# A first stage rewritten around one pass per tile: scaling, squares and h without GpSimd arithmetic

## The chip, the cores and the metric

The kernel runs on one core of one Trainium2 chip. The metric is the device time of one execution in microseconds (us), lower is better; it is given as the median of several runs. Engines are named as in the profile: PE (TensorE matmul) and PEld (its weight load), DVE (VectorE), ACT (ScalarE), POOL (GpSimd), SP (SyncE, which here only issues transfers).

## The reference: what is computed

One layer of a hybrid decoder for a prompt of 1024 tokens and 8 samples of 8 tokens (1088 tokens in all), width 1024, all in fp32. Cut to what the change touches:

```
mod = silu(c) @ w_mod + b_mod
shift, scale, gate = split(mod, 3)
h = rmsnorm(x, norm_g) * (1 + scale) + shift
proj = h @ w_in                      # columns mg, u, va, za, q, k, v, o, z, gates, p, zc
...                                  # three token mixers, gated and merged
x = x + gate * (merged @ w_out);  y = rmsnorm(x, final_norm_g)
```

The prompt has one c, so one shift and scale a channel; each sample has its own, so there are nine columns of them (`[:, 0]` for the prompt, `[:, 1:9]` for the samples).

## The kernel before, in words

Activations lie transposed: channels on the 128 partitions (8 tiles, index k), the T = 1088 tokens along the free dimension, the 1024 prompt tokens first (`TP`), then the 64 of the samples (`smp`). Every fp32 product is made of three products of fp32r parts: a number is split into a high part (a cast, on ACT) and a low part (the number minus its high part, on DVE), and high x high, high x low and low x high are summed. `split` is this pair of operations. A panel is 256 columns of a weight matrix; `Stream` brings its four pieces (128x512) by SP and splits them (`step`: `whi` on ACT, L132, `wlo` on DVE, L101).

The first stage (`start`) works before shift and scale are known. It writes q = ((x * am) @ w) * r + shift @ w, where am is norm_g * (1 + scale) and r the reciprocal root mean square of a token. So panels q0 and q1 are multiplied with x * am, without r and shift; these are put in afterwards. Meanwhile r is computed, and h = x * am * r + shift is built, for panels q2, q3 and all that follow.

The order of all this is written by hand: `PLAN_0` and `PLAN_1` are strings whose letters name operations, and each engine carries out its instructions in the order in which the letters issue them. The letters: `1` load of a panel of w_mod (1 MB in slots of 128x1024), `2` load of an x tile (544 KB), `3` load of a weight piece, `w` a few dummy matmuls, `S` split of half a w_mod panel (`ssh`, `ssl`), `M` its product with the silu(c) columns `scs` (16 matmuls, L548), `C` copy out of PSUM (L554), `T` turn into am or sm (shift) columns (L564, L569, L571), `Q` square of an x tile (L577, L580) and its addition to `acc` (POOL, L581), `A`/`V` scaling of x by am in place (samples L586, prompt on ACT L588 or DVE L590), `H`/`L` high and low part of the scaled x (L595, L601), `W` split of a weight piece, `P`/`R` high and low passes of one x tile against q0 or q1 (12 and 6 matmuls, L614), `e` sum of squares over channels (matmuls L625) and r (`rs`; its power runs on POOL, L217, the refinement on DVE), `f` r spread over partitions (`rb`, L641, L644), `v`/`g` x * rb on DVE or POOL (L648), `m` high and low part of h with the shift added on the way (L653 to L660; the upper halves of the first four tiles are also stored to `b12d`), `z`/`s`/`t` the product shift @ w for q0 and q1 (L668 to L690), `r` the raw sums out of PSUM into rows (L698, L700).

The pool of SBUF slots has 34 buffers of 128x1088; x tiles, splits, h and rows all live there. PSUM has 8 banks in this stage.

After the plan come panels q2 (`b_panel`, six sums of 24 matmuls, L270) and q3. In q3 (`kouter=True`) the loop over k is the outer one: six sums fill six banks and are copied out together at the end (`evac_rows`, L859). Beside the two panels run generators, one step at a time (`tick`): `finish_rows` multiplies the rows of q0 and q1 by rb on POOL (L705), adds the shift term and stores them; `gen_factors` prepares right-hand factors for the panels after them. Those (`seven_panels`, matmuls L362) are computed with seven half-size products for eight; their factors t1 to t4 are sums and differences of quarters of h, which `gen_factors` first puts together again as hh + hl (`fac`, L765). `put_t4` overwrites the upper half of h's first four tiles with the fourth of them. Later, `gen_gate` multiplies silu(c) (`self.scs`, kept since the start) with the last third of w_mod.

Of the kernel before, what the change touches and what calls it, by code (L numbers as in the profile page):

```python
# [16 lines left out]
TP = 1024  # L17
# [141 lines left out]
class Builder:  # L159
# [98 lines left out]
    def b_panel(self, panel, acts, evac, nk=KT, kouter=False, hook=None):  # L258
# [3 lines left out]
        units = [(f, g) for f in range(2) for g in range(3)]  # L262
# [22 lines left out]
        for u, (f, g) in enumerate(units):  # L285
            p = self.ps()
            for k in range(nk):
                mms(p, f, g, k)
                if k == nk // 2 - 1:
                    self.tick(self.pace / 2)  # L290
            evac(f, g, p[:, : GROUPS[g][1]])
            self.prep_some(panel, u, len(units))
            self.tick(self.pace / 2)
        self.st.used(panel)
# [171 lines left out]
    def start(self):  # L466
# [10 lines left out]
        raws, wsp, pmod, xs, xsp = {}, {}, {}, {}, {}  # L477
# [41 lines left out]
        A.copy(self.scs[:, :, 0:9], sc)  # L519
        V.tensor_tensor(out=self.scs[:, :, 32:41], in0=sc, in1=self.scs[:, :, 0:9].bitcast(F32), op=ALU.subtract)  # L520
# [9 lines left out]
        def mod_split():  # L530
            n, j = divmod(nxt("ms"), 2)
            raw = raws[n][j]
            hi = self.slot([128, 4, 256], F32R, name="ssh")
            lo = self.slot([128, 4, 256], F32R, name="ssl")
            m = 4 if n else 2
            for q in range(0, 4, m):
                self.split(*(x[:, q : q + m] for x in (raw, hi, lo)))
# [4 lines left out]
        def mod_mul():  # L542
            n = nxt("mm")
            p = pmod[n] = self.ps()
            w = wsp.pop(n)
            for kk in range(KT):
                for j in range(2):
                    PE.matmul(p[:64, :256], self.scs[:, kk, :], w[kk // 4][j][:, kk % 4, :],  # L548
                              start=(kk == 0 and j == 0), stop=(kk == KT - 1 and j == 1))
# [7 lines left out]
        def mod_turn():  # L557
# [3 lines left out]
            if n == 0:  # L561
                V.tensor_scalar(bmod[:, 1, :], bmod[:, 1, :], 1.0, None, ALU.add)
            for j in range(2):
                PE.matmul(p[:, j * 16 : j * 16 + 9], t[:, j * 128 : j * 128 + 128], sel, start=True, stop=True)  # L564
# [8 lines left out]
        def square():  # L573
# [4 lines left out]
            else:  # L578
                sq = self.slot([128, T], name="sq")
                A.activation(sq, xs[k], AF.Square)  # L580
                G.tensor_tensor(out=acc[0], in0=acc[0], in1=sq, op=ALU.add)  # L581

        def x_scale(on_act):
            k = nxt("xa")
            x = xs[k]
            V.tensor_tensor(out=bview(x[:, smp]), in0=bview(x[:, smp]), in1=bcol(am[:, k, 1:9]), op=ALU.mult)  # L586
            if on_act:
                A.activation(x[:, :TP], x[:, :TP], AF.Copy, scale=am[:, k, 0:1])  # L588
            else:
                V.tensor_scalar(x[:, :TP], x[:, :TP], am[:, k, 0:1], None, ALU.mult)  # L590

        def x_high():
            k = nxt("xh")
            hi = self.slot([128, T], F32R, name="xhi")
            A.copy(hi, xs[k])  # L595
            xsp[k] = [hi, None]

        def x_low():
            k = nxt("xlo")
            lo = self.slot([128, T], F32R, name="xlo")  # L600
            V.tensor_tensor(out=lo, in0=xs[k], in1=xsp[k][0].bitcast(F32), op=ALU.subtract)  # L601
            xsp[k][1] = lo

        def mms(part):
# [13 lines left out]
            if n == KT - 1 and part == "low":  # L618
                self.st.units -= 4

        def rms_sum():
            p = self.ps()
            for t in range(9):
                m = 128 if t < 8 else 64
                PE.matmul(p[:m, t : t + 1], acc[0][:, t * 128 : t * 128 + m], ones, start=True, stop=True)  # L625
            ms = self.const([128, 9], "ms")
# [5 lines left out]
            acc.clear()  # L632

        def rms_rows():
            rb.append(self.slot([128, T], name="rb"))
            for b in range(3):
                p = self.ps()
                n = 0
                for t in range(4 * b, min(9, 4 * b + 4)):
                    m = 128 if t < 8 else 64  # L640
                    PE.matmul(p[:, n : n + m], rs[:m, t : t + 1].to_broadcast([m, 128]), self.ident[:m, :m],  # L641
                              start=True, stop=True)
                    n += m
                A.copy(rb[0][:, b * 512 : b * 512 + n], p[:, :n])  # L644

        def h_scale(eng):
            x = xs[nxt("hs")]
            eng.tensor_tensor(out=x, in0=x, in1=rb[0], op=ALU.mult)  # L648

        def h_make():  # L650
            k = nxt("hm")
            x = xs.pop(k)
            V.tensor_tensor(out=bview(x[:, smp]), in0=bview(x[:, smp]), in1=bcol(sm[:, k, 1:9]), op=ALU.add)  # L653
            hh = self.slot([128, T], F32R, name="hhi")
            hl = self.slot([128, T], F32R, name="hlo")
            A.activation(hh[:, :TP], x[:, :TP], AF.Identity, bias=sm[:, k, 0:1])
            A.copy(hh[:, smp], x[:, smp])
            V.scalar_tensor_tensor(out=hl[:, :TP], in0=x[:, :TP], scalar=sm[:, k, 0:1], in1=hh[:, :TP].bitcast(F32),
                                   op0=ALU.add, op1=ALU.subtract)
            V.tensor_tensor(out=hl[:, smp], in0=x[:, smp], in1=hh[:, smp].bitcast(F32), op=ALU.subtract)  # L660
# [11 lines left out]
        def shift_mm():  # L672
# [20 lines left out]
        def raw_rows():  # L693
            r = [self.slot([128, T], name="row") for _ in range(2)]
            for u in range(6):
                f, (g0, n) = u // 3, GROUPS[u % 3]
                if u % 2:
                    V.tensor_copy(r[f][:, g0 : g0 + n], sums[-1][u][:, :n])  # L698
                else:
                    A.copy(r[f][:, g0 : g0 + n], sums[-1][u][:, :n])  # L700
            rows.append(r)

        def finish_rows(n):
            for f in range(2):
                G.tensor_tensor(out=rows[n][f], in0=rows[n][f], in1=rb[0], op=ALU.mult)  # L705
# [8 lines left out]
            if n:  # L714
# [3 lines left out]
        def late_const():  # L718
            self.ident = self.cload("ident")

        ops = {
            "1": mod_load, "2": x_load, "3": self.st.load, "4": late_const,
            "w": keep_warm, "S": mod_split, "M": mod_mul, "C": mod_copy, "T": mod_turn,
            "Q": square, "A": lambda: x_scale(True), "V": lambda: x_scale(False), "H": x_high, "L": x_low,
            "W": self.st.step, "P": lambda: mms("high"), "R": lambda: mms("low"),
            "e": rms_sum, "f": rms_rows, "v": lambda: h_scale(V), "g": lambda: h_scale(G), "m": h_make,
            "z": shift_split, "s": shift_mm, "t": shift_turn, "r": raw_rows,
        }
        self.st.ahead = 1
# [11 lines left out]
        self.drain()  # L741

        def hook(k):
            for j in range(2):
                if k == j + 1:
                    self.put_t4(j)
            if k in (1, 3):
                self.side = [self.gen_factors(2 + k // 2)]
            self.tick(2)
            if k in (5, 6):  # L750
                self.put_t4(k - 3)

        self.b_panel(self.pan["q", 3], self.h, self.evac_rows(3, self.qd), kouter=True, hook=hook)
        self.drain()
        self.pace = 1

    def gen_factors(self, j):
# [3 lines left out]
        ab = []  # L761
        for k in (j, j + 4):
            hh, hl = self.h[k]
            t = self.slot([128, T], name="fac")
            V.tensor_tensor(out=t, in0=hh.bitcast(F32), in1=hl.bitcast(F32), op=ALU.add)  # L765
            ab.append(t)
            yield
        a, b = ab
        a0, a1, b0, b1 = a[:, :W], a[:, W:], b[:, :W], b[:, W:]
        V.tensor_tensor(out=a0, in0=a1, in1=a0, op=ALU.subtract)  # L770
        V.tensor_tensor(out=a1, in0=b1, in1=a1, op=ALU.subtract)
        V.tensor_tensor(out=b1, in0=b1, in1=a0, op=ALU.subtract)
# [3 lines left out]
        self.split(a, *t13)  # L776
        if j % 2 == 0:
# [72 lines left out]
    def evac_rows(self, n, dst, scale=None):  # L850
# [3 lines left out]
        def evac(f, g, ps):  # L854
            g0, w = GROUPS[g]
            if g == 0:
                st[f] = self.slot([128, T], name="row")
            if scale is None:
                self.A.copy(st[f][:, g0 : g0 + w], ps)  # L859
            else:  # L860
                self.A.mul(st[f][:, g0 : g0 + w], ps, scale)
            if g == 2:
# [1102 lines left out]
```

## Time and profile before

| | us |
|---|---|
| median of 3 runs (lowest, highest) | 1856.58 (1855.35, 1859.59) |
| the profiled execution | 1857.86 |
| its span, first to last instruction | 1856.1 |
| busy in the span: PE, DVE, ACT, POOL | 1796.1, 1071.9, 586.0, 262.3 |
| mean granted clock of PE | 0.985 of full speed |
| panel q2 begins; the seven-product panels begin | 119.3; 176.9 |

In the rows that follow, a group row reads: line, engine, operation, output <- inputs, shapes, count, then busy us and mean ns of one, then the idle time of the engine just before these instructions and what ended it. A row of the time line or of the chain begins with the start in us and the duration. A row of stretches gives for each engine the busy time and in brackets the number of instructions, then the granted PE clock, the share of DMA engines busy and GB/s.

### The profile page before, as it was taken

What the parts mean: (1) busy time and instruction counts of PE and PEld (TensorE: products, weight loads), DVE (VectorE), ACT (ScalarE), POOL (GpSimd) and SP (SyncE); (2) the same over time, 40 slices, a digit from 0 to 9 for tenths busy, and PEclk for the clock granted to TensorE, in tenths of its full rate; (3) what the DMA queues carried; (4) which work ended last, traced back from release to release, by engine and by line L of the source; (5) the groups of instructions that cost most, each with busy time, mean ns of one, the idle gap of its engine ahead of it and who ended that gap; (6) DMA issues with size and microseconds to landing.
All of it is one profiled execution on the core that took longest, in us unless ns stands there. A gap on an engine that the chain in (4) does not pass through costs nothing.

```text
span 1856.1 us, 32242 instructions
## 1 busy us (share of the span) xinstructions
PE 1796.1 (97%) x13017; PEld 1777.4 (96%) x13017; DVE 1071.9 (58%) x2003; ACT 586.0 (32%) x1141; POOL 262.3 (14%) x427
## 2 busy tenths in 40 slices
PE   7888999999999999999999999999999999999998
PEld 7888999999999998999999899999999999999998
DVE  7777556665666542434527955664655766564444
ACT  5443333333333332222223125332333231131224
POOL 3440000000000001110011212321101101200023
PEclk8988999999999999999999999999999999999999
DMA  6332323332222334333335754776457577694422
GB/s 252 108 128 74 106 94 94 104 122 80 71 70 76 130 106 150 121 123 101 94 116 189 217 180 125 240 237 201 143 175 231 179 228 208 184 317 142 151 62 97
DMA packets 142152, 270.42 MB, mean 146 GB/s; under 512 B 19377, under 2 KB 66161, under 8 KB 142003
## 3 DMA queue, kind: packets, MB, share of 16 engines
q1 hardware_dynamic: 118786, 184.20, 31.4%
q0 software_dynamic: 23072, 83.91, 13.3%
q8 instruction: 102, 1.67, 0.4%
q14 instruction: 48, 0.39, 0.1%
q10 hardware_dynamic: 144, 0.26, 0.0%
HBM read 179.96 MB, written 88.35 MB: 145 GB/s over the span
## 4 chain that ended last, share of the span: by engine, by line
PE 86%; DVE 8%; issue 2%; DMA 2%; ACT 1%; POOL 1%; SPq 0%; POOLq 0%; DVEq 0%; ACTq 0%
PE ps L270 30%; PE ps L308 15%; PE p L362 8%; PE y L362 8%; PE z L362 8%; PE x L362 4%; PE ps L614 2%; PE ps L316 1%; PE ps L1466 1%; PE ps L1264 1%; PE ps L1485 1%; PE ps L1682 1%; PE ps L1439 1%; PE ps L1468 1%; DMA ss<-in_w_mod_dram 1%
## 5 line engine op out<-in xcount | busy, mean ns | idle before, releaser
L101 DVE TENSOR_TENSOR wlo<-raw,whi 128x512 fp32r<-128x512 f32 (+1 forms) x272 | 189.7, 698 | 115.6 <-ACT whi L132 115.6
L308 PE MATMUL ps<-whi,hhi 128*128 128x256 f32 (+1 forms) x768 | 218.5, 284 | 0.0
L308 PE MATMUL ps<-wlo,hhi 128*128 128x256 f32 (+1 forms) x768 | 216.0, 281 | 0.0
L308 PE MATMUL ps<-whi,hlo 128*128 128x256 f32 (+1 forms) x768 | 215.1, 280 | 0.0
L270 PE MATMUL ps<-hhi,whi 128*128 128x362 f32 (+1 forms) x624 | 208.2, 334 | 5.5 <-DVE C L1494 3.4
L270 PE MATMUL ps<-hlo,whi 128*128 128x362 f32 (+1 forms) x624 | 207.0, 332 | 1.9 <-DMA hlo<-b12d 1.7
L270 PE MATMUL ps<-hhi,wlo 128*128 128x362 f32 (+1 forms) x624 | 206.6, 331 | 0.0
L270 PE MATMUL ps<-yhi,whi 128*128 128x362 f32 (+1 forms) x576 | 190.1, 330 | 3.0 <-DVE mgr L1742 1.6
L270 PE MATMUL ps<-yhi,wlo 128*128 128x362 f32 (+1 forms) x576 | 188.7, 328 | 0.0
L270 PE MATMUL ps<-ylo,whi 128*128 128x362 f32 (+1 forms) x576 | 188.5, 327 | 0.0
L132 ACT CAST whi<-raw 128x512 fp32r<-128x512 f32 (+1 forms) x272 | 162.3, 617 | 44.9 <-DVE raw L123 36.3
L308 PEld LDWEIGHTS ps<-whi,hhi 128*128 128x128 f32 x768 | 144.6, 188 | 0.8 <-issue 0.4
L308 PEld LDWEIGHTS ps<-wlo,hhi 128*128 128x128 f32 x768 | 144.7, 188 | 0.0
L308 PEld LDWEIGHTS ps<-whi,hlo 128*128 128x128 f32 x768 | 144.4, 188 | 0.0
L270 PEld LDWEIGHTS ps<-hhi,whi 128*128 128x128 f32 x624 | 119.2, 191 | 6.7 <-DVE C L1494 3.6
L362 PE MATMUL p<-hhi,whi 128*128 128x272 f32 x400 | 116.1, 290 | 7.3 <-ACT row L859 7.3
L270 PEld LDWEIGHTS ps<-hlo,whi 128*128 128x128 f32 x624 | 119.5, 191 | 2.6 <-DMA hlo<-b12d 2.6
L270 PEld LDWEIGHTS ps<-hhi,wlo 128*128 128x128 f32 x624 | 119.4, 191 | 0.0
L362 PE MATMUL p<-hlo,whi 128*128 128x272 f32 x400 | 116.5, 291 | 0.0
L362 PE MATMUL p<-hhi,wlo 128*128 128x272 f32 x400 | 116.3, 291 | 0.0
L132 ACT CAST whi<-sum 128x512 fp32r<-128x512 f32 x75 | 46.6, 621 | 219.7 <-DVE sum L119 144.0
L270 PEld LDWEIGHTS ps<-yhi,whi 128*128 128x128 f32 x576 | 108.2, 188 | 3.7 <-DVE mgr L1742 1.8
(434 smaller groups left out, 4489.6 us busy)
## 6 DMA issues: line engine op xcount, KB each, us to landing
raw<-in_w_in_dram SPq DMA_DIRECT2D x204, 256.0 KB
mgr<-mgd SPq DMA_DIRECT2D x24, 544.0 KB
raw<-in_w_br_dram SPq DMA_DIRECT2D x48, 256.0 KB
out_dram<-C POOLq DMA_DIRECT2D x36, 256.0 KB, 4.5
ylo<-yd SPq DMA_DIRECT2D x16, 544.0 KB
merd<-mgr POOLq DMA_DIRECT2D x16, 544.0 KB, 6.1
C<-in_state_C_dram SPq DMA_DIRECT2D x32, 256.0 KB
mgd<-mg POOLq DMA_DIRECT2D x14, 544.0 KB, 4.6
```

Of the source, the lines that this page charges most:

```text
L101: self.kb.V.tensor_tensor(out=lo, in0=src, in1=hi.bitcast(F32), op=ALU.subtract)
L132: kb.A.copy(hi, src)
L270: self.PE.matmul(ps[:, :n], part(panel, w, k, fs), a[:, g0 : g0 + n], start=(k == 0 and j == 0), stop=(k == nk - 1 and j == 2))
L308: self.PE.matmul(p[:, :cols], a[:, ts], part(panel, w, k, cs), start=(k == 0 and j == 0), stop=(k == KT - 1 and j == 2))
L316: self.PE.matmul(p[:, :cols], stack[:, k, :], part(panel, j, k, cs), start=(k == 0 and j == 0), stop=(k == KT - 1 and j == 1))
L362: PE.matmul(bank[n][:, g, :HT], w[:, ks], b[:, gs], start=(n in (1, 5, 6, 7) and j == 0 and m == 0), stop=(j == 3 and m == 2), skip_group_ ...
L614: PE.matmul(sums[-1][u][:, :m], self.st.part(w, 1 - ww, k, fs), a[:, g0 : g0 + m], start=(k == 0 and part == "high" and j == 0), stop=(k = ...
L1264: self.PE.matmul(p[:, :n], wsl[:, ww, k, fs], a[:, g0 : g0 + n], start=(k == 0 and j == 0), stop=(k == 1 and j == 2))
L1439: PE.matmul(x["ps"][:, h * 128 : h * 128 + 128], k[:, 2 * h + d, :], q[:, 2 * h + d, :], start=(d == 0), stop=(d == 1))
L1466: PE.matmul(p[:, :258], x["qw"][:, 2 * h + d, :], C[x["hp"]][:, h, d, :], start=(d == 0), stop=False)
L1468: PE.matmul(p[:, :258], x["P"][:, a, h, :], x["vs"][:, b, h, :], start=(x["c"] == 0 and j == 0), stop=(j == 2))
L1485: PE.matmul(p[:, :258], x["ks"][:, a, h, d * 128 : d * 128 + 128], x["vs"][:, b, h, :], start=(j == 0), stop=(j == 2))
```

## The change

- x is no longer scaled in place for the prompt: `H` scales while it casts (ACT), `L` forms x * am - high in one scalar-tensor-tensor (DVE). The samples' 64 columns are scaled in place inside `H`. Letters `A` and `V` go.
- The squares are added on DVE, and each h scale is on DVE as x * am * rb in one operation; `m` adds the shift into x in fp32 (ACT) and then splits it. x stays alive as fp32 h, and `gen_factors` takes it from there, without hh + hl.
- `e` also makes the place for rb; `f` comes in two parts. The row sums of q1 are multiplied by rb while they leave PSUM (DVE), those of q0 on DVE in `finish_rows`; the turn of the shift product moves there too.
- q3 runs in the order of `b_panel` with the sums in the order 2, 1, 0, 5, 4, 3, each copied out when it is done; `put_t4` follows in a hook after each sum.
- The plan is another: loads, splits and products of a group stand together; the first w_mod panel comes in two loads, the small loads ahead of it. `gen_gate` builds its own `scs`.

```diff
         def mod_load():
-            m = 4 if n else 2
-            for j in range(0, KT, m):
-                S.dma_start(raws[n][j // 4][:, j % 4 : j % 4 + m], i["w_mod"][panels[n]][:, j : j + m, :])
+            for j in range(2):
+                S.dma_start(raws[n][j], i["w_mod"][panels[n]][:, 4 * j : 4 * j + 4, :])
...
-        cT = self.slot([128, KT, 9], name="cT")
+        cT = self.const([128, KT, 9], "cT")
         S.dma_start(cT, i["cT"])
-        mod_load()
-        sel = self.cload("sel")
         bmod = self.cload("bmodT")
         ng = self.cload("norm_gT")
...
                 A.activation(sq, xs[k], AF.Square)
-                G.tensor_tensor(out=acc[0], in0=acc[0], in1=sq, op=ALU.add)
-        def x_scale(on_act):
-            ...
+                V.tensor_tensor(out=acc[0], in0=acc[0], in1=sq, op=ALU.add)
         def x_high():
-            A.copy(hi, xs[k])
+            A.activation(hi[:, :TP], x[:, :TP], AF.Copy, scale=am[:, k, 0:1])
+            V.tensor_tensor(out=bview(x[:, smp]), in0=bview(x[:, smp]), in1=bcol(am[:, k, 1:9]), op=ALU.mult)
+            A.copy(hi[:, smp], x[:, smp])
         def x_low():
-            V.tensor_tensor(out=lo, in0=xs[k], in1=xsp[k][0].bitcast(F32), op=ALU.subtract)
+            V.scalar_tensor_tensor(out=lo[:, :TP], in0=x[:, :TP], scalar=am[:, k, 0:1], in1=hi[:, :TP].bitcast(F32),
+                                   op0=ALU.mult, op1=ALU.subtract)
+            V.tensor_tensor(out=lo[:, smp], in0=x[:, smp], in1=hi[:, smp].bitcast(F32), op=ALU.subtract)
...
-        def h_scale(eng):
-            eng.tensor_tensor(out=x, in0=x, in1=rb[0], op=ALU.mult)
+        def h_scale():
+            V.scalar_tensor_tensor(out=x[:, :TP], in0=x[:, :TP], scalar=am[:, k, 0:1], in1=rb[0][:, :TP], op0=ALU.mult,
+                                   op1=ALU.mult)
+            V.tensor_tensor(out=x[:, smp], in0=x[:, smp], in1=rb[0][:, smp], op=ALU.mult)
+            V.tensor_tensor(out=bview(x[:, smp]), in0=bview(x[:, smp]), in1=bcol(sm[:, k, 1:9]), op=ALU.add)
         def h_make():
-            x = xs.pop(k)
-            V.tensor_tensor(out=bview(x[:, smp]), in0=bview(x[:, smp]), in1=bcol(sm[:, k, 1:9]), op=ALU.add)
-            A.activation(hh[:, :TP], x[:, :TP], AF.Identity, bias=sm[:, k, 0:1])
-            A.copy(hh[:, smp], x[:, smp])
-            V.scalar_tensor_tensor(out=hl[:, :TP], in0=x[:, :TP], scalar=sm[:, k, 0:1], in1=hh[:, :TP].bitcast(F32),
-                                   op0=ALU.add, op1=ALU.subtract)
-            V.tensor_tensor(out=hl[:, smp], in0=x[:, smp], in1=hh[:, smp].bitcast(F32), op=ALU.subtract)
+            x = xs[k]
+            A.activation(x[:, :TP], x[:, :TP], AF.Identity, bias=sm[:, k, 0:1])
+            self.split(x, hh, hl)
...
         def raw_rows():
-                if u % 2:
-                    V.tensor_copy(r[f][:, g0 : g0 + n], sums[-1][u][:, :n])
+                if rows:
+                    V.tensor_tensor(out=d, in0=sums[-1][u][:, :n], in1=rb[0][:, g0 : g0 + n], op=ALU.mult)
+                elif u % 2:
+                    V.tensor_copy(d, sums[-1][u][:, :n])
...
         def finish_rows(n):
-            for f in range(2):
-                G.tensor_tensor(out=rows[n][f], in0=rows[n][f], in1=rb[0], op=ALU.mult)
+            shift_turn()
             yield
             for f in range(2):
+                if n == 0:
+                    V.tensor_tensor(out=r, in0=r, in1=rb[0], op=ALU.mult)
...
-        self.side = [finish_rows(0), finish_rows(1), self.gen_factors(0), self.gen_factors(1)]
+        self.side = [finish_rows(0), finish_rows(1)] + [self.gen_factors(j) for j in range(4)]
...
-        self.b_panel(self.pan["q", 3], self.h, self.evac_rows(3, self.qd), kouter=True, hook=hook)
+        self.b_panel(self.pan["q", 3], self.h, self.evac_rows(3, self.qd), hook=hook, order=(2, 1, 0, 5, 4, 3))
...
     def gen_factors(self, j):
-        for k in (j, j + 4):
-            hh, hl = self.h[k]
-            t = self.slot([128, T], name="fac")
-            V.tensor_tensor(out=t, in0=hh.bitcast(F32), in1=hl.bitcast(F32), op=ALU.add)
-            ...
+        a, b = self.xs.pop(j), self.xs.pop(j + 4)
...
 Builder.PLAN_0 = (
-    "wSS3w21M2W2CT1QVwSH4SL2wPQMV2Q1CWTHR21VSPHLSPMQ3Q2RVHLRLCTPVWSRHL23SPWQQMC3RVTHAHLLwPRQV3H"
-    "LPSSRPR1WS3"
+    "1223w 1223wQQSSwMCTHHWLLw SSMC1223QQTPHHWPLLRR SSMC1223QQTPHHWPLLRR SSMC13QQTPHHWPLLRR 13WPPRRe"
 )
 Builder.PLAN_1 = (
-    "rW13SeSM1CPP3MS3PCfRTSgMCgPWSvRgTMgCRTvRTPzmWRmsmgPmPWmWgPRRmtms3R3WmW3tr"
+    "r3WPR 1SSMCPRffTvm 1SSMCPRWvmPRT SSMC3vmPRWvmPRT SSMC3vmPRvmPRTzs 3vm3vmsWWWWr"
 )
```

More of the change, by code (lines that the diff above doesn't have):

```diff
@@ L255, in prep_some, with b_panel @@
                 self.st.step()
-    def b_panel(self, panel, acts, evac, nk=KT, kouter=False, hook=None):
+    def b_panel(self, panel, acts, evac, nk=KT, kouter=False, hook=None, order=(0, 1, 2, 3, 4, 5)):
         self.st.need(panel)
         part = self.st.part
-        units = [(f, g) for f in range(2) for g in range(3)]
+        units = [divmod(u, 3) for u in order]
         def mms(ps, f, g, k):
@@ L293, in b_panel @@
             self.tick(self.pace / 2)
+            if hook is not None:
+                hook(u)
         self.st.used(panel)
@@ L531, in mod_split @@
             n, j = divmod(nxt("ms"), 2)
-            raw = raws[n][j]
             hi = self.slot([128, 4, 256], F32R, name="ssh")
             lo = self.slot([128, 4, 256], F32R, name="ssl")
-            m = 4 if n else 2
-            for q in range(0, 4, m):
-                self.split(*(x[:, q : q + m] for x in (raw, hi, lo)))
+            self.split(raws[n][j], hi, lo)
             wsp.setdefault(n, []).append((hi, lo))
@@ L547, in mod_mul @@
                 for j in range(2):
-                    PE.matmul(p[:64, :256], self.scs[:, kk, :], w[kk // 4][j][:, kk % 4, :],
-                              start=(kk == 0 and j == 0), stop=(kk == KT - 1 and j == 1))
+                    PE.matmul(p[:64, :256], scs[:, kk, :], w[kk // 4][j][:, kk % 4, :], start=(kk == 0 and j == 0),
+                              stop=(kk == KT - 1 and j == 1))
         def mod_copy():
@@ L617, in mms, with rms @@
                 xsp[k] = None
-            if n == KT - 1 and part == "low":
-                self.st.units -= 4
-        def rms_sum():
+        def rms():
             p = self.ps()
@@ L631, in rms_sum @@
             self.rsqrt(rs, ms, rt)
-            acc.clear()
+            rb.append(self.slot([128, T], name="rb"))
         def rms_rows():
[L635 to L644, printed above, removed]
@@ L646, in h_scale @@
-        def h_scale(eng):
-            x = xs[nxt("hs")]
-            eng.tensor_tensor(out=x, in0=x, in1=rb[0], op=ALU.mult)
+            b = nxt("rr")
+            t0, t1 = ((0, 4), (4, 9))[b]
+            ps = [self.ps() for _ in range(-(-(t1 - t0) // 4))]
+            for t in range(t0, t1):
+                m = 128 if t < 8 else 64
+                o = (t - t0) % 4 * 128
+                PE.matmul(ps[(t - t0) // 4][:, o : o + m], rs[:m, t : t + 1].to_broadcast([m, 128]), self.ident[:m, :m],
+                          start=True, stop=True)
@@ L776, in gen_factors @@
         self.split(a, *t13)
+        yield
         if j % 2 == 0:
@@ L855, in evac @@
             g0, w = GROUPS[g]
[L856 to L862, printed above, removed]
-                self.G.dma_start(dst[2 * n + f], st.pop(f))
+            if f not in st:
+                st[f] = [self.slot([128, T], name="row"), 0]
+            self.A.copy(st[f][0][:, g0 : g0 + w], ps)
+            st[f][1] += 1
+            if st[f][1] == 3:
+                self.G.dma_start(dst[2 * n + f], st.pop(f)[0])
         return evac
@@ L882, in load @@
             return w
+        scs = self.slot([128, KT, 64], F32R, name="scs")
+        V.tensor_copy(scs, self.zero.unsqueeze(1).to_broadcast([128, KT, 64]))
+        self.A.copy(scs[:, :, 0:9], self.sc)
+        V.tensor_tensor(out=scs[:, :, 32:41], in0=self.sc, in1=scs[:, :, 0:9].bitcast(F32), op=ALU.subtract)
         nxt = load(0)
```

93 lines of the change are left out of this document (44 added, 49 removed).

## The prediction

> **What bounds the kernel now.** I read the engine line of the page, then the busy times of the stretches around the change, then the chain that ended last in order of time, then the groups of each engine in the first 177 us.
>
> ```profile
> PE 1796.1 (97%) x13017; PEld 1777.4 (96%) x13017; DVE 1071.9 (58%) x2003; ACT 586.0 (32%) x1141; POOL 262.3 (14%) x427
> ...
> core 0: us, PE busy (x) PEld busy (x) DVE busy (x) ACT busy (x) POOL busy (x), PEclk, DMA share, GB/s
> 0.00:60.16 60.16, 47.81 (x304) 44.28 (x305) 46.55 (x52) 34.73 (x42) 20.82 (x14) 0.89 0.60 216
> 60.16:119.31 59.15, 47.25 (x301) 45.02 (x301) 45.75 (x57) 22.64 (x40) 29.05 (x17) 0.90 0.34 114
> 119.31:176.87 57.56, 50.29 (x290) 49.99 (x289) 44.63 (x60) 24.77 (x42) 8.86 (x9) 0.92 0.25 87
> 176.87:336.87 160.00, 160.00 (x1253) 160.00 (x1254) 84.92 (x129) 52.73 (x89) 7.97 (x15) 0.98 0.33 108
> ```
>
> The first row says TensorE: 97% busy over the span. The stretches say where it is not. From 176.87 us on (the seven-product panels) PE has no gap; the 32 us that it idles before that, and the clock below 1, all lie in the first stage. Whatever the change does to the time, it does by moving the moment at which those panels start. The chain gives the marks:
>
> ```profile
> 106.25 7.89 DVE x L653
> ...
> 119.38 22.41 PE ps L270 x120
> ...
> 174.64 2.18 ACT row L859 x6
> 176.87 5.78 PE p L362 x24
> ...
> 191.72 3.01 PE p L362 x24
> ```
>
> Panel q2 starts at 119.38 and the seven-product panels at 176.87. Ahead of the latter stand six row copies (L859) that nothing covers, and behind that gap the first 24 matmuls took 5.78 us where later ones take 3.01. An addition over 128x64 (L653) held the chain for 7.89 us. The groups say why:
>
> ```profile
> L208 DVE TENSOR_TENSOR ssl<-ss,ssh 128x1024 fp32r<-128x1024 f32 x14 | 20.1, 1441 | 3.2 <-ACT ssh L207 3.2
> L101 DVE TENSOR_TENSOR wlo<-raw,whi 128x512 fp32r<-128x512 f32 x18 | 15.8, 879 | 5.8 <-ACT whi L132 5.7
> L601 DVE TENSOR_TENSOR xlo<-x,xhi 128x1088 fp32r<-128x1088 f32 x8 | 12.5, 1569 | 1.7 <-ACT xhi L595 1.7
> L658 DVE SCALAR_TENSOR_TENSOR hlo<-x,sm,hhi 128x1024 fp32r<-128x1024 f32 x8 | 10.2, 1278 | 4.4 <-ACT hhi L656 4.3
> L590 DVE TENSOR_SCALAR x<-x,am 128x1024 f32<-128x1024 f32 x7 | 9.8, 1395 | 0.0
> L653 DVE TENSOR_TENSOR x<-x,sm 128x64 f32<-128x64 f32 x8 | 9.5, 1184 | 0.0
> L586 DVE TENSOR_TENSOR x<-x,am 128x64 f32<-128x64 f32 x8 | 6.8, 846 | 0.7 <-ACT acc L577 0.7
> L569 DVE TENSOR_SCALAR am<-ps,c_bmodT,c_norm_gT 128x9 f32<-128x9 f32 x8 | 1.9, 280 | 3.5 <-PE ps L564 3.5
> ...
> L590 DVE TENSOR_SCALAR x<-x,am x7: 739/746/3026, 12.0 to 55.1; 128x1024 f32<-128x1024 f32 x7
> ...
> L586 DVE TENSOR_TENSOR x<-x,am x8: 210/220/2558, 11.8 to 52.7; 128x64 f32<-128x64 f32 x8
> ...
> L581 POOL TENSOR_TENSOR acc<-acc,sq 128x1088 f32<-128x1088 f32 x7 | 20.4, 2913 | 33.8 <-ACT sq L580 33.5
> L648 POOL TENSOR_TENSOR x<-x,rb 128x1088 f32<-128x1088 f32 x6 | 17.8, 2987 | 5.9 <-ACT rb L644 5.8
> L705 POOL TENSOR_TENSOR row<-row,rb 128x1088 f32<-128x1088 f32 x4 | 10.0, 2514 | 0.0
> L217 POOL TENSOR_TENSOR rs<-ms,mhalf 128x9 f32<-128x9 f32 x1 | 1.8, 1819 | 11.7 <-DVE ms L630 11.7
> ```
>
> The min/median/max rows of L590 and L586 show the same operation at 0.75 and 3.03 us, and at 0.22 and 2.56 us: the long ones are longer by about one GpSimd operation (2.5 to 3.0 us). So DVE stands still while GpSimd works. On L586, L590 and L653 that is 8 x (0.846 - 0.220) + 7 x (1.395 - 0.746) + 8 x (1.184 - 0.220) = 17 us; other lines add to it.
>
> **The change, part by part.** The engines work in the order written: the DVE, ACT and PE rows stand in the plan's order. So I walk the new plan through the queues with these rows:
>
> ```profile
> 25.18 1.21 DVE L208 TENSOR_TENSOR ssl<-ss,ssh 128x1024 fp32r<-128x1024 f32 x1
> 26.31 1.28 DVE L601 TENSOR_TENSOR xlo<-x,xhi 128x1088 fp32r<-128x1088 f32 x1
> ...
> L207 ACT CAST ssh<-ss 128x1024 fp32r<-128x1024 f32 x14 | 14.6, 1049 | 4.9 <-PE ps L614 3.0 <-DVE ssl L208 1.1 <-DMA ss<-in_w_mod_dram 0.8
> L132 ACT CAST whi<-raw 128x512 fp32r<-128x512 f32 x18 | 11.0, 618 | 3.4 <-DVE raw L123 2.3 <-DMA raw<-in_w_in_dram 1.1
> L656 ACT ACTIVATE hhi<-x,sm 128x1024 fp32r<-128x1024 f32 x8 | 9.2, 1147 | 0.0
> L595 ACT CAST xhi<-x 128x1088 fp32r<-128x1088 f32 x8 | 8.8, 1098 | 12.8 <-DVE x L590 12.8
> L554 ACT COPY smp<-ps 64x256 f32<-64x256 f32 x8 | 2.9, 364 | 12.8 <-PE ps L548 12.7
> ...
> 45.35 1.83 PE ps L548 x16
> ...
> 69.97 1.98 PE ps L614 x12
> 71.95 2.15 PE ps L641 x18
> ...
> 10.67 1.11 ACT L577 ACTIVATE acc<-x 128x1088 f32<-128x1088 f32 x1 [0.72 <-DMA x<-in_xT_dram]
> ...
> 60.16 2.04 PE L625 MATMUL ps<-ones,acc 128*128 128x1 f32 x18
> ...
> 35.35 1.91 PE L614 MATMUL ps<-xlo,whi 128*128 128x364 f32 x6 [3.80 <-DVE xlo L601]
> ...
> 47.02 1.15 PE L614 MATMUL ps<-xlo,whi 128*128 128x364 f32 x6
> ...
> 57.07 0.44 PE L614 MATMUL ps<-xhi,whi 128*128 128x364 f32 x1 [1.57 <-ACT xhi L595]
> ```
>
> Neighbours on an engine overlap by some 0.08 us (26.31 - 25.18 = 1.13 for an operation of 1.21); I take that off. Without GpSimd beside it a DVE subtraction is worth 1.21 us (128x1024) or 1.28 (128x1088), a weight split 0.62 on ACT and about 0.68 on DVE (a plain 128x512), a scalar-tensor-tensor 1.28.
>
> *Opening.* Both squares now stand ahead of the first split of the modulation weights on ACT, so the first split waits for x tile 1. Before, 1.87 MB (modulation panel 0, one weight piece, x tile 0) had landed by 10.67. Now 2.16 MB must land, and three small loads go ahead of them on SP: between 10.6 (nothing) and 12.2 (0.29 MB at the 0.18 MB/us that 1.87 MB in 10.67 us makes); I take 11.4. Panel 0 coming in two loads and not four costs nothing beside that, as its split waits for the squares anyway. Then in a row: square 1.1, addition 1.2, two subtractions 2.35, the second half of the modulation product (8 of the 16 matmuls of L548, 1.0 at full clock, 2.0 at half), copy 0.4, turn 0.5 (four small matmuls, as 2.15 / 18 each) to 1.0, am 0.5, two scaled highs 2.4, weight high 0.6 and low 0.65, two lows 2.7. The first group ends at 25 to 26.
>
> *Groups two to four* (letters SSMC...QQT.HHW.LL). Every step waits for the one before it on another engine: subtractions 2.35, second half of the product 1.05, copy 0.35, square 1.05, two additions 2.5, am 0.45, highs 2.4, weight high 0.6, weight low 0.65, lows 2.6. That is about 14.0 us a group, and the next group's subtractions stand behind the lows on DVE. PE has 1.83 + 0.5 + 2 x 1.98 + 2 x 1.0 = 8.3 us of work in it, so it idles over 4 us a group. The modulation product and both passes over q0 for six of the eight tiles are done 42 us later: 67 to 68. The seven additions that leave GpSimd (7 x 2.91) come back as 7 x 1.28 = 9 us on DVE inside this chain; the 7 x 1.395 = 9.8 us of L590 go, since the scaling rides in operations that exist (ACT high 1.10 to 1.15, low 1.28 for an uncontended 1.28).
>
> *To the row sums and back.* The last two tiles wait for q0's fourth piece (weight low some 11 us into group four); then 6 us of matmuls, the sums 2.04: they end near 72, where they began at 60.16. The rsqrt keeps its GpSimd power (1.82 us); DVE waits there, and three of the six row copies (1.4 on DVE; six on ACT took 2.18) stand behind it, 76.
>
> *Second part.* The first round runs through two subtractions, half a product, q1's matmuls 3.0, the spread of the row factors 2.15, its ACT copy 0.7, h scale 1.5, and h made in three steps that alternate ACT 1.15, ACT 1.10, DVE 1.28: 92. Before, the high came straight out of the bias pass, so the fp32 h costs one more ACT pass of 1.10 a tile in the chain. The three further rounds take 10.2, 12.9 and 13.3 us with sm and the shift's split: 128. The shift's product (1.83 + 0.37) is copied on ACT ahead of tile 6, which waits for it: 130.5. Tiles 6 and 7 take 3.3 and 4.8, the first q2 piece 0.6. Panel q2 can start at 139, against 119.38.
>
> *Clock.* The 12-matmul pass and the six-matmul pass show that PE restarts slowly: after 3.80 us idle six matmuls took 1.91 us, in a busy stretch 1.15, and after 1.57 us the first shows 0.44 and no more. The new plan leaves gaps of 3.2 to 7 us ahead of seven of the eight modulation products and the shift's product, and these are in the chain. Half a product at half clock and the wait for its first half cost about 1.4 each, the shift's 1.6: at most 10 us in all, at least 0. The gaps are nearer to 3.80 than to 1.57, so I take 8: q2 at 147.
>
> [...]
>
> *q2 and q3.* Their 288 matmuls at 0.165 (1.98 / 12) take 47.6, the slow restart 2.3, the two shift turns between them 1.1, the end 1.0: 52, against 57.5. The additions hh + hl of the factors (8 x 1.28 on DVE) are gone, but DVE has 44.6 less 10 and plus 6 for the rows, 40 us of work under these 52, so that alone gives nothing; what gives is that q3 no longer keeps six banks to its end, so one copy instead of six stands ahead of the next stage. If DVE fell behind there (its row product needs rb and the banks first, 6 x 0.55), some 3 us would come back. The seven-product panels start at 147 + 52 = 199, against 176.87: 22 us late. Their first matmuls no longer come out of a 7 us gap, which returns 5.78 - 3.01 = 2.8. Rebuilding the gate's 512-wide factor later is under 1 us of DVE beside busy PE: nothing. POOL's queue keeps only its transfers and the power; the b12d and row transfers go out earlier on it, and nothing in the stage waits for them.
>
> **Sum**: 27.6 later at q2, 5.5 back in q2/q3, 2.8 back behind it: +19.3. The profiled execution took 1857.86 (span 1856.1 and 1.8 around it), 1.3 above the median of 1856.58; so 1877 by its own time and 1876 by the median.
>
> **Rivals.** *DVE gives all of its time back* (faster). If DVE is what is fed last, as in 106.25, the end follows its work: the stage has 137 us of DVE work in three rows above; 17 of blocked time go at least, 10 of the additions hh + hl, 10 of L590, and 9 of squares, 9 of scaling and 3 of rows come. That is 16 less, and the new ending of q3 adds 8: 1834. It needs PE and ACT to stay a group ahead of DVE; then DVE would have to be busy over 80% in the first 60 us. Against it: in the new order DVE's subtractions for one panel wait behind lows that wait for that same group's product, so nothing can be ahead. [...]
>
> *A wash.* No clock penalty, x at 10.6, the rounds each 0.5 us shorter (8 + 0.8 + 7 x 0.5): 1864; to reach 1860 or less something must overlap that I placed in a row.
>
> *Loads held back.* Slots are scarcer in the second part (x stays until the factors): modulation panels 6 and 7 can be issued only as others come free, and the weight loads stand behind them on SP. They have 15 us to spare; held longer than that, each 5 us late shows in full: 1885 to 1895.
>
> **How the numbers follow.** The serial chain with most restarts slow, 1864 to 1887: 0.71, time 1876. Loads held back: 0.09. A wash within 0.2% (3.7 us, about what a measurement can tell): 0.07. DVE gives all back: 0.13. The range 1861 to 1888 leaves out the faster rival and the far end of the held loads. Faster 0.13, same 0.07, slower 0.80.
>
> **What would show it.** Row sums (the 128x1 matmuls) near 72 to 78 and the first q2 matmul near 147, seven-product panels near 199; DVE operations of the stage all at their short duration, no arithmetic on POOL but the power; PE waiting once a group for the low of the modulation weights, about 14 to 15 us apart, at a clock below 1; the six-copy gap gone. Wrong it is if those products follow each other in 11 us or less, or if DVE is above 80% busy up to the row sums.

## The result and the profile after

| | before | after |
|---|---|---|
| median of 4 runs each (lowest, highest), us | 1856.04 (1855.35, 1859.59) | 1886.96 (1884.11, 1888.91) |
| the profiled execution; its span | 1857.86; 1856.1 | 1884.11; 1882.1 |
| first matmul of panel q2; of the seven-product panels | 119.31; 176.87 | 152.45; 204.44 |

The changed kernel is slower: ratio 1.0161, 95% interval 1.0142 to 1.0181. First the engine line of the page after and the busy times by stretch. The first of those rows are groups two, three and four, each from the last low of one group to the last low of the next; then come the three further rounds of the second part, the stretch to q2, and panels q2 and q3.

```profile
PE 1805.5 (96%) x13009; PEld 1784.3 (95%) x13009; DVE 1047.9 (56%) x2014; ACT 591.5 (31%) x1144; POOL 211.1 (11%) x410
...
26.66:42.06 15.40, 12.57 (x56) 11.84 (x56) 8.87 (x14) 7.27 (x10) 0.00 (x0) 0.67 0.19 77
42.06:57.31 15.25, 10.39 (x56) 9.47 (x56) 8.87 (x14) 7.27 (x10) 0.00 (x0) 0.89 0.26 86
57.31:72.77 15.46, 13.73 (x64) 13.30 (x65) 8.87 (x15) 5.89 (x9) 0.00 (x0) 0.67 0.52 171
...
98.92:113.38 14.46, 12.41 (x57) 11.33 (x56) 6.27 (x10) 6.08 (x7) 1.64 (x3) 0.67 0.29 103
113.38:127.14 13.76, 10.34 (x56) 9.74 (x56) 8.84 (x14) 6.80 (x8) 1.62 (x3) 0.88 0.19 66
127.14:140.41 13.27, 10.02 (x55) 9.70 (x55) 8.23 (x13) 5.15 (x6) 0.54 (x1) 0.87 0.09 37
140.41:153.60 13.19, 6.49 (x35) 5.76 (x35) 7.00 (x13) 7.00 (x11) 0.00 (x0) 0.71 0.00 0
153.60:204.44 50.84, 50.29 (x295) 49.49 (x295) 35.09 (x54) 21.69 (x36) 3.74 (x7) 0.97 0.35 124
```

In a group of 15.4 us DVE is busy for 8.9, ACT for 5.9 to 7.3, and PE for 10.4 to 13.7 at a granted clock of 0.67 to 0.89: no engine is busy throughout. Each waits for another in turn. In the second group PE waits 3.1 us for DVE's low, ACT for PE's product, and DVE for the square and then for the weight high of ACT:

```profile
31.44 0.36 ACT L553 COPY smp<-ps 64x256 f32<-64x256 f32 x1 [6.18 <-PE ps L547]
...
32.85 2.69 DVE L578 TENSOR_TENSOR acc<-acc,sq 128x1088 f32<-128x1088 f32 x2 [3.83 <-ACT sq L577]
...
38.79 0.69 DVE L101 TENSOR_TENSOR wlo<-raw,whi 128x512 fp32r<-128x512 f32 x1 [2.60 <-ACT whi L132]
```

Before, DVE was busy 46.6 us of the 60.2 ahead of the row sums; here it is busy 36.1 us of 77.3.

The chain that ended last has marks like those of before, and says what stood at each. The row of 152.45 is from PE's time line: q2's first two matmuls run there, then PE waits once more for a weight low, and the chain's q2 starts at 153.60.

```profile
104.87 7.66 PE ps L608 x36
112.53 0.55 PE ps L561 x4
...
141.44 2.77 PE ps L674 x16
...
152.45 0.67 PE L270 MATMUL ps<-hhi,whi 128*128 128x364 f32 x1 [5.50 <-ACT whi L132]
...
153.60 3.11 PE ps L270 x10
...
157.25 6.16 PE ps L270 x36
...
204.44 3.30 PE p L364 x24
```

q2's first matmul comes 33.1 us later than before and the seven-product panels begin 27.6 later. Behind that mark the rest of the span is 1677.7 us, against 1679.2 (1882.1 - 204.44 and 1856.1 - 176.87). So 5.6 us come back in q2 and q3, 1.6 behind them, and the spans differ by 26.0. The medians differ by 30.9. Of the other 4.9, 4.7 lie between the runs: the profiled execution of before is 1.8 above its median, that of after 2.9 below.

What PE waited for in the first 205 us, in total, times and longest:

```profile
PE ps L547 <- ACT ssh L207: 17.6, 5, 6.4
PE ps L547 <- DVE ssl L208: 15.7, 10, 3.2
...
PE p L364 <- ACT row L847: 0.6, 1, 0.6
```

The same view of before, for the product that is L548 there:

```profile
PE ps L548 <- DVE ssl L208: 2.1, 1, 2.1
```

33 us of waits stand ahead of one kind of instruction, the modulation product (L547), whose halves wait for the split. Before, this product waited for a low once, 2.1 us. The last row is what is left of the wait ahead of the seven-product panels. And GpSimd is indeed out of DVE's way; the small products and additions that took 0.85 and 1.18 us on average before (L586 and L653 there) are short, and so are the additions of squares that are DVE's now:

```profile
L578 DVE TENSOR_TENSOR acc<-acc,sq 128x1088 f32<-128x1088 f32 x7 | 9.0, 1292 | 20.3 <-ACT sq L577 20.0
...
L648 DVE TENSOR_TENSOR x<-x,sm 128x64 f32<-128x64 f32 x8 | 1.8, 225 | 0.3
...
L585 DVE TENSOR_TENSOR x<-x,am 128x64 f32<-128x64 f32 x8 | 1.4, 217 | 0.0
```

So the operations did what they say, and the time was lost between them. The theory: the order of the letters makes the loss, and the new operations by themselves gain. The rivals: PE's slow clock makes it, or the work that went from GpSimd to DVE, or the new ending of q3 hides more or less than it seems.

### The profile page after: what moved, and what is told of

It reads as the page before. It is cut to its first block, busy times and chain, and to the rows that moved or that the text cites. A ratio compares the mean times of both kernels' runs of the same rounds, so it can differ in the third digit from the quotient of the medians.

```text
span 1882.1 us, 32195 instructions
## 1 busy us (share of the span) xinstructions
PE 1805.5 (96%) x13009; PEld 1784.3 (95%) x13009; DVE 1047.9 (56%) x2014; ACT 591.5 (31%) x1144; POOL 211.1 (11%) x410
## 4 chain that ended last, share of the span: by engine, by line
PE 84%; DVE 5%; issue 2%; ACT 2%; DMA 1%; POOL 1%; SPq 0%; POOLq 0%; DVEq 0%; ACTq 0%
PE ps L270 31%; PE ps L310 15%; PE z L364 8%; PE y L364 8%; PE p L364 8%; PE x L364 4%; PE ps L318 1%; PE ps L1456 1%; PE ps L1254 1%; PE ps L1475 1%; PE ps L1672 1%; PE ps L1429 1%; PE ps L1458 1%; DVE va L1009 1%; DMA hlo<-b12d 0%
```

## Experiments

**The new operations in an order that feeds the engines (e1_plan).** Only the two plan strings of the changed kernel differ: the split of the next panel stands ahead of the lows of the group before, and its product directly behind that group's high passes. In the second part both h scales come first in a round, the halves of the split stand between the shifts, and the turn (T) stands ahead of the weight passes (P), not behind them. One of the dummy-matmul letters is gone.

```diff
-    "1223w 1223wQQSSwMCTHHWLLw SSMC1223QQTPHHWPLLRR SSMC1223QQTPHHWPLLRR SSMC13QQTPHHWPLLRR 13WPPRRe"
+    "1223w1223wSSwMCQQTW HHSS1223LLPPMCTQQWRR HHSS1223LLPPMCTQQWRR HHSS13LLPPMCTQQWRR HHSS13LLPPWRRe"
-    "r3WPR 1SSMCPRffTvm 1SSMCPRWvmPRT SSMC3vmPRWvmPRT SSMC3vmPRvmPRTzs 3vm3vmsWWWWr"
+    "MCr3WTffPRPR 1vvSmSmMCTWPRPR 1vvSmSmMCT3WPRPR 3vvSmSmMCTPRPR zs3vvWmWm3sWWr"
```

> The changed kernel with the same letters in another order: SS and LL of neighbouring groups interleaved, the turn ahead of the squares, both h scales of a round ahead of the splits that hide the ACT passes. No operation is added or removed but one idle filler. Theory 1 (each letter waits for the one before it on another engine; the plan's order is the loss): the spacing of the modulation products falls from 15.3 us to about 10 in the first part and from 13.7 to about 9.5 in the second, panel q2 begins 30 us earlier, 1887 goes to 1848 to 1865. Theory 2 (the operations themselves cost the time, above all those that came to DVE): the spacing stays above 13 us and the time above 1879.

Measured: 1841.43 us, ratio to before 0.992 (0.9905 to 0.9935): a larger gain than theory 1 allowed. Its chain:

```profile
114.66 6.91 PE ps L270 x34
...
162.59 3.30 PE p L364 x24
```

The seven-product panels begin 41.9 us earlier than in the changed kernel. (The first row is not the start of q2: its first matmul runs at 108.55, and PE waits for weight pieces of q2 in between.) The time line of DVE gives the period of the second part by its shift operation (L568):

```profile
89.07 0.36 DVE L568 TENSOR_SCALAR sm<-ps,c_bmodT 128x9 f32<-128x9 f32 x2
...
98.87 0.36 DVE L568 TENSOR_SCALAR sm<-ps,c_bmodT 128x9 f32<-128x9 f32 x2 [0.86 <-PE ps L561]
```

That is 9.8 us a round (98.87 - 89.07), where the changed kernel took 13.3 to 14.5 for the same operations. In the first part the groups still took 10.4 to 12.3 us (am, L566, to am), not the 10 that was expected. With the operations the same, the order decides, and not the work moved to DVE. The clock goes with the order: PE's granted clock from the row sums to the chain's q2 was 0.99 here (62.41 to 114.66) and 0.82 in the changed kernel (77.33 to 153.60).

**A second order (e6_plan2).** As e1_plan, but in the first part the split and the product of a group come ahead of the scaled highs, and only the copy and the turn stay behind the lows.

```diff
-    "... HHSS1223LLPPMCTQQWRR HHSS1223LLPPMCTQQWRR HHSS13LLPPMCTQQWRR HHSS13LLPPWRRe"
+    "... SSMHH1223LLPCQTQWPRR SSMHH1223LLPCQTQWPRR SSMHH13LLPCQTQWPRR SSHH13LLPPWRRe"
```

> The changed kernel's operations with the reordered plan of e1_plan, whose first part is ordered once more: both splits of the next modulation panel and its product stand ahead of the two x highs, so that DVE has the splits to do while ACT makes the highs. In e1_plan the first part still had 12.2 us a group with some 2.3 us of DVE waiting for ssh and 2.3 more for the turn. Theory 1: about 9.7 us a group (DVE's own work is 8.7), 7 us less in all: 1831 to 1838. Rival (loads or PE set the first part by now): 1839 to 1843.

Measured: 1833.12 us, ratio 0.9861 (0.984 to 0.9882), within what was expected. This is the best version found: 26 us under before (0.0139 x 1856) and 54 under the changed kernel. Its chain and, in the second fence, the waits of PE that were 17.6 and 15.7 us:

```profile
52.28 1.90 PE ps L617 x18
...
104.53 8.41 PE ps L270 x34
...
153.97 3.30 PE p L364 x24
```

```profile
PE ps L547 <- ACT ssh L207: 4.2, 2, 2.4
PE ps L547 <- DVE ssl L208: 3.8, 5, 1.5
```

The row sums begin at 52 us and not at 77.33. What q2 still lost here, 8.41 us for 34 matmuls where e1_plan took 6.91 (5.6 at the 0.165 of the prediction), was not followed up.

**The old operations in the new order (e7_oldops).** The kernel before, its operations placed as the changed plan places them (the scaling V ahead of each high, the h scales on GpSimd and VectorE as before; one scaling goes from ACT to DVE, one weight load and one `w` fewer are in the plan, and `4` is the load of a constant).

```diff
-    "wSS3w21M2W2CT1QVwSH4SL2wPQMV2Q1CWTHR21VSPHLSPMQ3Q2RVHLRLCTPVWSRHL23SPWQQMC3RVTHAHLLwPRQV3H"
-    "LPSSRPR1WS3"
+    "223w 1223wQQSSwMCTVHVHWLLw SSMC1223QQTPVHVHWPLLRR SSMC1223QQTPVHVHWPLLRR 4SSMC13QQTPVHVHWPLLRR 13WPPRRe"
-    "rW13SeSM1CPP3MS3PCfRTSgMCgPWSvRgTMgCRTvRTPzmWRmsmgPmPWmWgPRRmtms3R3WmW3tr"
+    "r3WPR 1SSMCPRfTgm 1SSMCPRWgmPRT SSMC3vmPRWgmPRT SSMC3vmPRgmPRTzst 3gm3gmstWWWWr"
```

> The operations of the kernel before (x scaled in place on DVE, squares, six h scales and the row products on GpSimd, hh + hl, q3 in six banks) in the changed kernel's order of letters, with a V ahead of each H and the shift's turn behind each s. Theory 1 (the order makes the loss): 1880 to 1905. Theory 2 (the operations that were changed make it): 1852 to 1866.

Measured: 1895.65 us, ratio 1.0199 (1.0181 to 1.0217), as theory 1 had it. What PE waited for:

```profile
PE ps L548 <- DVE ssl L208: 19.4, 11, 3.0
PE ps L548 <- ACT ssh L207: 18.8, 6, 5.6
```

The same two waits as in the changed kernel, with none of its new operations. Four ratios to before now stand together: old operations in their own order 1, in the new order 1.0199; new operations in the new order 1.0161, in a feeding order 0.9861. The order costs the old operations 2%; the new ones give 0.4% back in that order (the two intervals touch), and together with an order that suits them they are 1.4% faster than before. The old operations in that last order were not run, so what it is worth to them is open.

**No arithmetic on GpSimd, nothing else changed (e3_nopool).** In the kernel before the seven square additions, six h scales and four row products go to VectorE; the rsqrt's power stays.

```diff
-                G.tensor_tensor(out=acc[0], in0=acc[0], in1=sq, op=ALU.add)
+                V.tensor_tensor(out=acc[0], in0=acc[0], in1=sq, op=ALU.add)
-                G.tensor_tensor(out=rows[n][f], in0=rows[n][f], in1=rb[0], op=ALU.mult)
+                V.tensor_tensor(out=rows[n][f], in0=rows[n][f], in1=rb[0], op=ALU.mult)
-            ... "g": lambda: h_scale(G), "m": h_make,
+            ... "g": lambda: h_scale(V), "m": h_make,
```

> The kernel before with its own plan and operations, only the GpSimd arithmetic goes to DVE: seven additions of squares, six h scales, four row products. DVE takes 17 x 1.28 = 22 us more of work and loses some 33 us of standing still. Theory A (the stalls beside GpSimd were in the chain): DVE shortens by about 11 us and the time by 4 to 11: 1845 to 1852. Theory B (DVE was fed late anyway, and the squares make it wait in order): 1856 to 1866. The share of the change's loss that comes from moving arithmetic to DVE is read from it.

Measured: 1838.75 us, ratio 0.9902 (0.9885 to 0.9918): a gain larger than expected, and most of e6_plan2's 1.4%, with the old order. The groups of DVE in the first 177 us:

```profile
L590 DVE TENSOR_SCALAR x<-x,am 128x1024 f32<-128x1024 f32 x7 | 5.2, 747 | 0.0
...
L586 DVE TENSOR_TENSOR x<-x,am 128x64 f32<-128x64 f32 x8 | 1.7, 219 | 0.3 <-ACT acc L577 0.3
L653 DVE TENSOR_TENSOR x<-x,sm 128x64 f32<-128x64 f32 x8 | 1.7, 217 | 0.0
```

Before, their means were 1395, 846 and 1184 ns. DVE took on 7 x 1.29 + 6 x 1.29 + 4 x 1.28 = 22 us of work and the kernel became 18 us faster (0.0098 x 1856). So DVE's stalls beside GpSimd were in before's chain, more than the expectation allowed. The chain of before bears this out; in the second fence stands what POOL did while the 128x64 addition held the chain from 106.25 for 7.89 us, a mean of 1184 ns being one such operation and seven short ones:

```profile
28.86 2.95 DVE x L590
...
84.56 3.53 DVE x L648
```

```profile
106.64 2.53 POOL L648 TENSOR_TENSOR x<-x,rb 128x1088 f32<-128x1088 f32 x1
...
109.13 4.92 POOL L705 TENSOR_TENSOR row<-row,rb 128x1088 f32<-128x1088 f32 x2
```

With the like pieces at L601 (3.50), L208 (3.52), L586 (2.56) and L660 (2.56) and the one at L653, these are some 21 us above the short durations ahead of q2. No operation of POOL itself stands in the chain there, so nothing in it supports the rival that the kernel waited for GpSimd's own slow operations.

**Squares only, in the kernel before (e5_sq) and back in the changed one (e8_poolsq).**

```diff
# e5_sq, in the kernel before; e8_poolsq is the reverse edit in the changed kernel
-                G.tensor_tensor(out=acc[0], in0=acc[0], in1=sq, op=ALU.add)
+                V.tensor_tensor(out=acc[0], in0=acc[0], in1=sq, op=ALU.add)
```

> The kernel before with one of the three GpSimd parts alone moved to DVE: the seven additions of squares. DVE takes 9 us of work and is rid of the stalls at L586, L590 and L601 (12 us above their uncontended durations). If those stalls were in the chain: 3 to 9 us less, 1847 to 1853. If the gain of e3_nopool lies in the second part alone (h scales and rows): 1855 to 1859.

Measured: 1851.47 us, ratio 0.9965 (0.9952 to 0.9979), within what was expected. The addition ahead of h still takes its long time, as the h scales are on GpSimd still:

```profile
L653 DVE TENSOR_TENSOR x<-x,sm 128x64 f32<-128x64 f32 x8 | 9.5, 1186 | 0.0
```

About a third of e3_nopool's gain is the squares'; by difference, the rest belongs to the h scales and the rows.

> The changed kernel with one part undone: the seven additions of squares go back to GpSimd, all else in its own order. Two additions (2.5 us) leave each group's chain between the squares and the am columns, but the GpSimd additions (2 x 2.6 to 2.9 us) then stand beside the DVE operations that follow. Theory 1 with the stalls: the lows start hardly earlier, 0.5 to 2 us a group, 1878 to 1885. If moving the squares to DVE was itself the loss: below 1877. If the stalls weigh more: above 1888.

Measured: 1881.12 us, ratio 1.0125 (1.0109 to 1.0141), within what was expected. DVE's groups up to the row sums show the block again:

```profile
L585 DVE TENSOR_TENSOR x<-x,am 128x64 f32<-128x64 f32 x8 | 7.1, 914 | 0.7 <-ACT sq L577 0.7
```

The mean is 0.914 us and not 0.217; yet the kernel is 6 us faster than the changed one. A reading that fits, and that no run isolates: in that order the additions stand in the serial chain on DVE, and a second engine is worth more than an unblocked one. The traces show 1.8 us of the 6, ahead of the row sums (75.50 for 77.33); the rest is not located. The same edit thus gains 0.35% in one order and loses 0.36% in the other.

**Dummy matmuls against the slow clock (e2_warm).** More of the letter `w` in the changed kernel's plan, at the gaps of PE; they compute nothing that is used.

```diff
-    "1223w 1223wQQSSwMCTHHWLLw SSMC1223QQTPHHWPLLRR SSMC1223QQTPHHWPLLRR ...
+    "1223w 1223wQQwwwwSSwwMCTHHWLLwwww SSMC1223QQTPHHWPLLRRwwwww SSMC1223QQTPHHWPLLRRwwwww ...
-    "r3WPR 1SSMCPRffTvm 1SSMCPRWvmPRT SSMC3vmPRWvmPRT SSMC3vmPRvmPRTzs 3vm3vmsWWWWr"
+    "r3WPR 1SSMCPRffTvmwwwwww 1SSMCPRWvmPRT SSMC3vmPRWvmPRTwwwww SSMC3vmPRvmPRTwwwwzs 3vm3vmsWWWWr"
```

> The changed kernel with dummy matmuls (letter w) put into the gaps ahead of seven of the eight modulation products and ahead of the shift's product; nothing else moves. Theory 1 with the restarts of PE in the chain: the products run at a clock near 1, each 1.0 to 1.4 us shorter, 8 to 10 us in all: 1877 to 1879. Theory 2 (the slow clock lies beside other work): within 2 us of 1887. If the dummies stand in the way: above 1889.

Measured: 1883.09 us, ratio 1.0143 (1.0128 to 1.0158). Its chain:

```profile
147.77 3.40 PE ps L270 x10
...
152.13 7.82 PE ps L270 x36
...
200.97 3.30 PE p L364 x24
```

That lies between the two theories. q2's first matmul comes 5.8 us earlier (146.63), but after the first ten of the chain the next 36 took 7.82 us where they took 6.16: the slow stretch moved. 3.9 us of the median remain, half of the 8 that the prediction put on the restarts, and the intervals of the two ratios overlap. The gaps were filled only in part: PE still waited 19.4 us (10.9 and 8.5) for the halves of the split, where it waited 33.3, and the mean granted clock of the span rose from 0.977 to 0.984, half of the way to the 0.991 of e1_plan. If 5.8 us go with that half, all of it would be some 12 us; this is an estimate. q2 still came 27.3 us later than before. So the clock is a part of the loss and not the whole of it.

**q3's new ending alone (e4_q3).** The kernel before with the sums of q3 in the new order, each copied out when done; the factors are still made by hh + hl.

```diff
-        self.b_panel(self.pan["q", 3], self.h, self.evac_rows(3, self.qd), kouter=True, hook=hook)
-        self.drain()
+        self.side = [self.gen_factors(2), self.gen_factors(3)]
+        self.b_panel(self.pan["q", 3], self.h, self.evac_rows(3, self.qd), hook=hook, order=(2, 1, 0, 5, 4, 3))
```

> The kernel before with one part of the change alone: panel q3 in six sums one after the other (order 2, 1, 0, 5, 4, 3), each copied out when done, instead of six banks copied at the end; hh + hl for the factors is kept. Theory 1: the 7.3 us gap ahead of the seven-product panels falls to about 1 and their first 24 matmuls from 5.8 to 3.3 us: 1847 to 1850. Rival (DVE, which keeps hh + hl, is then late with the factors): the gap stays as a wait for DVE, 1853 or more.

Measured: 1855.95 us, ratio 0.9995 (0.9986 to 1.0005): no gain. The gap did not fall to 1 us; the rival that was named, DVE late with the factors, came true. PE's wait ahead of the seven-product panels:

```profile
PE p L364 <- ACT row L858: 4.4, 1, 4.4
```

The wait is 4.4 us; in the changed kernel it is 0.6. The chain ahead of it here is the factors' additions and their splits on DVE, so the copies were late for that reason. In the changed kernel, where the fp32 h takes the additions hh + hl away, the 50.84 us row has PE busy for 50.29. So the ending seems to pay together with the fp32 h; the fp32 h without the new ending was not run.

## Why the prediction was right, and where it was off

The forecast was 1876 us with a range up to 1888; 1886.96 was measured, a loss of 26.0 us by the spans and 30.9 by the medians for a sum of 19.3. The direction and the mechanism were right. That the time fell inside the range was in part luck: its middle was 11 us short, and the slowest of the four runs, 1888.91, lies outside it.

**The mechanism held.** The bound was placed at the moment at which the seven-product panels start, and behind it the two kernels differ by 1.6 us. The serial chain of a group was put at 14.0 us, with about 1.4 for a slow restart: 15.4, 15.25 and 15.46 were measured. Row sums were put at 72 to 78 and began at 77.33. The 3.30 us row is the returned cost of the old gap: 5.78 - 3.30 = 2.5 of 2.8. The whole return behind the mark was 1.6. The three small signs came too: short DVE operations, no arithmetic on POOL but the power, and the six-copy gap gone. The signs of being wrong did not come: the products followed each other in 15 us and not in 11, and DVE was 47% busy up to the row sums (36.1 of 77.3), not 80%.

**q2 and q3** took 51.99 us from the first matmul (204.44 - 152.45) and were put at 52, from 57.5. The reason given, fewer copies and nothing for the additions hh + hl, is not borne out: in e4_q3 the new ending alone brought this stretch to 54.61 us (118.64 to 173.25) and the median nothing, since DVE with those additions came last. How the two share the 5.6 us is open.

**The step that was mis-sized** is the way to q2: it was put 27.6 us later than before and came 33.1 later. The walk without its clock term had the second part's first round end at 92, and it ended at 98.92, 6.9 us later, which five restarts at 1.4 would fill. The round after it put the walk 11.2 us behind (102.2, measured 113.38), the third further round 12.0 (128.4 by its own terms, measured 140.41), q2 13.5 (139, measured 152.45), where 8 had been allowed. So most of the 5.5 us that are missing lie in the first of the three further rounds: 10.2 us, measured 14.46. With its slow half product it would be 11.6, so 2.9 are missing. The ACT row shows a wait that was not in the sum: the split of the second half of the panel stood until the subtraction of the first half was done. It reads nothing that this subtraction writes, so what it waited for was, as far as the program shows, an SBUF slot that the subtraction freed; this is inferred.

```profile
100.17 1.04 ACT L207 CAST ssh<-ss 128x1024 fp32r<-128x1024 f32 x1 [1.55 <-DVE ssl L208]
```

Behind it PE ran 36 matmuls in 7.66 us (5.9 at the 1.98 for 12 of the prediction's row) ahead of the turn (L561), and DVE stood for that:

```profile
113.10 0.36 DVE L568 TENSOR_SCALAR sm<-ps,c_bmodT 128x9 f32<-128x9 f32 x2 [1.75 <-PE ps L561]
```

The 1.7 us by which the passes were slow are what DVE stood for. The prediction had put the slow clock on the products alone; here it also lengthened passes that the plan puts ahead of the turn. The other two rounds took 13.76 and 13.27 for 12.9 and 13.3, which with 1.4 each for the clock is 0.5 and 1.4 too much: the walk is better in its sum than step by step. The first group ended at 26.66 for 25 to 26.

The bound on the clock was added up wrongly as well: seven products at 1.4 and the shift's 1.6 are 11.4 and not "at most 10". From the forecast's own 139 that gives 150.4, and q2 came at 152.45.

**The clock.** The prediction took 8, gap by gap. e2_warm had 5.8 us back at q2 and 3.9 in the median with the gaps filled in part, and the last section says why a price for each gap is not the right form.

**The rivals.** "Loads held back" did not cost what was put: SP did hold loads of w_mod for slots, up to 21.1 us at a time, but in the chain from 100 to 153 us no DMA stands. A wash did not come. "DVE gives all of its time back" (1834) fell for this kernel, on the ground that the prediction gave: nothing can be ahead. But e6_plan2 came out at 1833, with the same operations once the engines do stay ahead, and e3_nopool at 1839. So that rival was right that the operations hold such a gain. Its number is partly chance: it asked for DVE to be over 80% busy, and in e6_plan2 DVE was busy 37.8 us of the 52.1 up to the row sums, 72%. Its premise, that DVE's operations take longer while GpSimd works, agrees with the means of the 128x64 addition (L653): 217 ns without (e3_nopool) and 1184 ns with GpSimd's h scales and row products (before).

**Open.** The slot wait was not tried by itself; nor was any part of e6_plan2's second part, where loads of weight pieces stand in the chain (8.0 and 3.0 us). The old operations, or those of e3_nopool, in the order of e6_plan2 were not run either: e3_nopool alone is 0.4% behind it.

## What to carry to other kernels

When engines take their instructions in order, read a rewritten plan as a chain through the queues: if each group's first step stands behind the last step of the group before on the same engine, the group costs the sum of its steps and not the largest, however cheap these have become (here 15.25 to 15.46 us a group, with no engine busy for more than 13.73). Cost the operations and the order apart, and try the new operations in an order that issues the next group's first steps early before giving them up. Work moved to an engine whose operations ran long beside that work can pay: without GpSimd's arithmetic the 128x64 additions of DVE took 217 ns and not 1184, and 22 us more work on DVE took 18 us off the kernel (e3_nopool).

## What the runs showed of the hardware that was not expected

The slow clock need not follow right behind a gap. In the changed kernel PE stood still for 1.32 us ahead of 114.65, started at full rate, and fell to half rate 0.6 us later; ahead of 141.44 it stood still for 3.01 us, started at full rate as well, and slowed 1.1 us into the product. From PE's time line (start, duration, and in brackets the idle time ahead; the starts are some 0.11 us apart at full rate and 0.21 at half):

```profile
114.65 0.33 PE L547 MATMUL ps<-ssl,scs 128*64 128x256 f32 x1 [1.32 <-DVE ssl L208]
...
115.28 0.40 PE L547 MATMUL ps<-ssh,scs 128*64 128x256 f32 x1
115.48 0.41 PE L547 MATMUL ps<-ssl,scs 128*64 128x256 f32 x1
...
118.61 0.38 PE L608 MATMUL ps<-xhi,whi 128*128 128x362 f32 x1
...
141.44 0.33 PE L674 MATMUL ps<-whi,scs 128*64 128x256 f32 x1 [3.01 <-DVE scs L666]
...
142.55 0.37 PE L674 MATMUL ps<-wlo,scs 128*64 128x256 f32 x1
142.72 0.41 PE L674 MATMUL ps<-whi,scs 128*64 128x256 f32 x1
...
145.92 0.33 PE L674 MATMUL ps<-wlo,scs 128*64 128x256 f32 x1
```

Both slow stretches lasted 3.3 to 3.4 us (115.28 to 118.61, 142.55 to 145.92). Both began inside busy matmuls; what sets the moment is not shown, and no run was made to test it. The shift's product, on which the prediction put 1.6 us for a slow restart, lost less: its 16 matmuls in the chain took 2.77 us, where 1.83 is full rate and 3.4 would be half (16 at 0.21).
